# A softmax router kernel: its first three loads moved from the kernel block to the entry block

## The chip, the cores and the metric

The program runs on one core of one Trainium2 chip. The metric is the device time of one execution in microseconds (us). Three unprofiled executions of the kernel before took 86.51, 86.59 and 86.63 us, so its time is the median, 86.59 us. One more execution was recorded by the hardware profiler: its device time was 86.38 us, and from its first to its last recorded instruction it spans 85.1 us.

## What is computed

```python
def setup_inputs():
    batch, seq, dim = 16, 512, 1024
    num_loras = 8
    # x: (16, 512, 1024) float32, router_weights: (1024, 8) float32

def reference(x, router_weights):
    logits = np.matmul(x, router_weights)
    exp_logits = np.exp(logits - np.max(logits, axis=-1, keepdims=True))
    return (exp_logits / np.sum(exp_logits, axis=-1, keepdims=True)).astype(np.float32)
```

There are 16 x 512 = 8192 rows of 1024 numbers. Each row is multiplied with eight columns of weights, and a softmax is taken over the eight results. The input is 33.55 MB and the output 0.26 MB.

## The kernel before

**Tiling.** The rows are laid over 128 partitions so that each partition holds 64 consecutive rows of x. A "row" of the kernel, index j from 0 to 63, is therefore 128 rows of x, one from each partition. The tile `xa` (named x_all in the profile) keeps all of x in bf16, 64 rows of 1024 numbers in each partition. Nothing is ever loaded twice, and no load waits for a buffer.

**Loads.** Rows 0 to 3 come in as float32: SyncE (SP) issues two transfers of two rows each into `x_f32` (lines 133 to 138, recorded as line 134), and ScalarE (ACT) issues the load of the weights into `w8` (line 140). They are written inside a block that the tile framework closes and compiles at lines 146 and 147, and each has its own semaphore: `s_f[0]`, `s_f[1]` and `s_w`. Rows 4 to 62 and the pieces of row 63 come through GpSimd's (POOL's) queue, which casts to bf16 on the way (lines 170 and 183). They follow the list `LOADS = [4] * 13 + [2, 2, 2] + [1] * 5` without its first entry: twelve transfers of four rows, three of two, five of one, and at last row 63 in three pieces of its columns, `PIECES = [4, 2, 2]` (in units of 128 columns). Between the second and the third of them POOL builds the identity matrix and a filler tile (lines 174 to 180).

**Work on a row.** ACT casts the four float32 rows to bf16 (line 337). For each row TensorE (PE) transposes eight 128 x 128 blocks (lines 233 and 278, the latter for all repeated ones), VectorE (DVE) copies five of them out of PSUM and ACT three (lines 395 and 351), and PE multiplies the eight transposed blocks with the weights (line 265 for the repeated ones, which include two filler matmuls in every two rows). After each eight rows DVE and ACT do the softmax. The last four rows are finished one by one, and two stores by SP write the result (lines 161 and 163).

**What sets the order.** Every engine has its instructions written out by hand, with semaphores between them. SP waits for each load in turn and counts the rows that are in into `s_in` (lines 152 to 158); PE takes one from `s_in` ahead of each row (lines 214 and 277). ACT waits for `s_f[0]` ahead of the first cast and for `s_f[1]` ahead of the third (line 335).

**The start of the program.** It has three blocks in a row that every engine goes through, and two of them hold barriers of all five engines.

1. The entry block, recorded under line 520: POOL writes four small constants, and each engine executes a drain and then joins a barrier.
2. The kernel block: the two float32 loads on SP and the load of the weights on ACT, and nothing else that is recorded.
3. The end of the tile block, recorded under line 147: drains, a barrier, a clearing of semaphores by POOL, drains, a second barrier. Behind it come the hand-written instructions of all engines, on POOL the first of the casting loads.

In a barrier POOL collects the arrivals of all the engines and then releases them.

Of the kernel before, what the change touches and what calls it, by code (L numbers as in the profile page):

```python
# [11 lines left out]
def kernel(  # L12
# [6 lines left out]
    nc = tc.nc  # L19
# [112 lines left out]
    with tc.manual_schedule():  # L132
        early = [
            nc.sync.dma_start(
                out=x_f32[:, 2 * i:2 * i + 2, :], in_=x_rows[:, 2 * i:2 * i + 2, :]
            ).then_inc(s_f[i], 16)
            for i in range(2)
        ]
# [6 lines left out]
            tc.no_tile_sem_insts.add(t.ins.name)  # L145
    tc.close()
    tc.compile()  # L147


    sp = nc.sync  # L150
# [120 lines left out]
    for n in range(N):  # L271
        t = pe.transpose(w_ps[:, n, :], w8[:, :, n], ident[0:KO, 0:KO])  # L272
# [263 lines left out]
```

## Time and profile before

| What | Value |
|---|---|
| Device time, median of three | 86.59 us (86.51 to 86.63) |
| Device time of the profiled execution | 86.38 us |
| Span of the profiled execution | 85.1 us |
| PE busy | 63.7 us (75%) |
| DVE busy | 39.5 us (46%) |
| ACT busy | 37.9 us (45%) |
| POOL busy | 13.4 us (16%) |
| Granted TensorE clock | 1.000 over the whole span |
| The two float32 loads: issued | 0.74 to 1.60 us, on SP |
| The load of the weights: issued | 0.74 to 1.33 us, on ACT |
| First casting load on POOL: issued | 3.29 us |
| First cast of a float32 row on ACT | 6.79 us |

A profile is one execution. "Busy" counts an engine's compute instructions; issuing a DMA, waiting and branching are not counted. Times in the profile count from the first recorded instruction, here a drain on SP in the entry block. The profile page also shows the span in 40 equal slices of 2.13 us, with the busy share of each engine and of the sixteen DMA engines in tenths. The rate in GB/s counts the bytes as they are written to their destination: a load that casts float32 to bf16 reads twice the bytes that it writes.

### The profile page before, as it was taken

Reading aid. Unit: us, or ns where it says so; the run is one execution under the profiler, and the core shown is the slowest. Engines: PE = TensorE matmul, PEld = TensorE weight load, DVE = VectorE, ACT = ScalarE, POOL = GpSimd, SP = SyncE. Lnnn points to the kernel's source line nnn. Section 1 sums busy time; section 2 is a strip of 40 time slices with the busy share of each in tenths; the row PEclk is TensorE's granted clock in tenths of the full one; section 3 lists DMA queues with packets and bytes.
Section 4 is the critical chain, followed back from the end, with each engine's and each line's share of the span. In section 5 each row is a group of like instructions: output and inputs, shape, how many; then the busy total and the mean of one; then the engine's idle time right before and its main releaser. Section 6 shows DMA issues by size and latency. Waiting matters only on the chain. (4 is left out here: it accounts for less than half of the span.)

```text
span 85.1 us, 2926 instructions
## 1 busy us (share of the span) xinstructions
PE 63.7 (75%) x1094; PEld 52.1 (61%) x1094; DVE 39.5 (46%) x114; ACT 37.9 (45%) x81; POOL 13.4 (16%) x30
## 2 busy tenths in 40 slices
PE   0044759999994977949596895949597799999760
PEld 0042648788774755838474674837476588777650
DVE  0021412377574442845265362736257257665661
ACT  0049683356453352535245262525336246555470
POOL 0489999800000000000000000000000000000000
PEclk9999999999999999999999999999999999999999
DMA  3899999899989999999999999999999999999920
GB/s 58 347 420 308 239 189 243 185 247 189 243 185 239 193 227 204 239 193 231 200 227 204 227 204 227 204 227 204 227 204 204 216 216 216 199 208 211 191 104 23
DMA packets 3904, 18.12 MB, mean 213 GB/s; under 512 B 568, under 2 KB 1080, under 8 KB 2112
## 3 DMA queue, kind: packets, MB, share of 16 engines
q0 software_dynamic: 3312, 15.73, 90.5%
q1 hardware_dynamic: 576, 2.36, 7.2%
q10 hardware_dynamic: 16, 0.03, 0.3%
HBM read 33.59 MB, written 0.26 MB: 398 GB/s over the span
## 5 line engine op out<-in xcount | busy, mean ns | idle before, releaser
L351 ACT COPY xTs<-pts 128x384 bf16<-128x384 bf16 x63 | 30.0, 476 | 37.5 <-PE pts L278 37.1
L395 DVE COPY xTv<-ptv 128x640 bf16<-128x640 bf16 x63 | 31.0, 492 | 32.3 <-PE ptv L278 29.7
L278 PE MATMUL ptv<-identity,x_all 128*128 128x128 bf16 x311 | 28.7, 224 | 12.7 <-PEq L214 11.4
L278 PEld LDWEIGHTS ptv<-identity,x_all 128*128 (+1 forms) x311 | 18.8, 99 | 14.1 <-issue 13.9
L278 PE MATMUL pts<-identity,x_all 128*128 128x128 bf16 x186 | 21.3, 225 | 0.0
L265 PEld LDWEIGHTS lg<-w_bf,xTv 128*128 128x128 bf16 x305 | 15.6, 98 | 7.8 <-issue 1.1
L265 PE MATMUL spare<-filler 128*128 128x512 bf16 x61 | 19.5, 402 | 0.4
L265 PE MATMUL lg<-w_bf,xTv 128*128 128x8 bf16 x305 | 16.6, 167 | 0.0
L278 PEld LDWEIGHTS pts<-identity,x_all 128*128 x186 | 13.6, 101 | 0.0
L265 PE MATMUL lg<-w_bf,xTs 128*128 128x8 bf16 x183 | 13.2, 166 | 0.0
L170 POOL DMA_DIRECT2D x_all<-in_x_dram x20 | 10.7, 612 | 2.8 <-POOLq L147 2.8
L265 PEld LDWEIGHTS lg<-w_bf,xTs 128*128 128x128 bf16 x183 | 9.0, 96 | 0.0
L265 PEld LDWEIGHTS spare<-filler 128*128 128x128 bf16 x61 | 4.4, 101 | 2.5 <-issue 2.5
L272 PE MATMUL lg<-ident,w 8*128 8x8 f32 x8 | 1.0, 251 | 5.3 <-PEq L270 5.3
L272 PEld LDWEIGHTS lg<-ident,w 8*128 8x128 f32 x8 | 0.9, 197 | 5.3 <-issue 5.3
L415 DVE TENSOR_REDUCE mx<-lg 128x8 f32 x8 | 1.8, 225 | 5.0 <-DVEq L465 4.5
L337 ACT CAST x_all<-x_f 128x1024 bf16<-128x1024 f32 x4 | 4.0, 1044 | 0.0
L337 ACT ACT_TABLE_LOAD x1 | 1.3, 1283 | 5.5 <-ACTq L335 5.5
L386 DVE CAST identity<-ident 128x128 bf16<-128x128 f32 x1 | 0.5, 518 | 5.3 <-POOL ident L176 5.3
L340 ACT ACTIVATE ev<-ex 128x64 f32<-128x64 f32 x8 | 2.0, 256 | 1.6 <-DVE ex L415 0.9
L431 DVE TENSOR_REDUCE ssum<-ev 128x8 f32<-128x64 f32 x8 | 1.8, 220 | 0.1
L415 DVE TENSOR_TENSOR ex<-lg,mx 128x64 f32<-128x64 f32 x8 | 1.7, 217 | 0.0
(41 smaller groups left out, 16.0 us busy)
## 6 DMA issues: line engine op xcount, KB each, us to landing
x_all<-in_x_dram POOLq DMA_DIRECT2D x12, 1024.0 KB, 32.1
x_f<-in_x_dram SPq DMA_DIRECT2D x2, 1024.0 KB, 6.3
x_all<-in_x_dram POOLq DMA_DIRECT2D x3, 512.0 KB, 59.9
x_all<-in_x_dram POOLq DMA_DIRECT2D x5, 256.0 KB, 64.0
out_dram<-out_all SPq DMA_DIRECT2D x1, 208.0 KB, 1.9
x_all<-in_x_dram POOLq DMA_DIRECT2D x1, 128.0 KB, 65.6
x_all<-in_x_dram POOLq DMA_DIRECT2D x2, 64.0 KB, 65.3
out_dram<-out_all SPq DMA_DIRECT2D x1, 48.0 KB, 1.6
```

Of the source, the lines that this page charges most:

```text
L170: nc.gpsimd.dma_start(out=xa[:, first[i]:first[i] + r, :], in_=x_rows[:, first[i]:first[i] + r, :]).then_inc(s_ld[i], 16)
L265: return pe.matmul(spare, lhsT=filler[:, 0:P], rhs=filler, start=True, stop=True)
L272: t = pe.transpose(w_ps[:, n, :], w8[:, :, n], ident[0:KO, 0:KO])
L278: turn_like = pe.transpose(turn_ap(0, 0), xa[:, 0, 0:P], identity).ins
L337: act.copy(xa[:, k, :], x_f32[:, k, :]).then_inc(s_cast, 1)
L340: return act.activation(ev, ex, func=Exp).then_inc(s_ev, 1)
L351: act.copy(xTs[j % 2], pts[j % 2][:, 0:SN, :]).then_inc(s_c[j % 2], 1)
L386: dve.tensor_copy(out=identity, in_=ident).then_inc(s_idb, 1)
L395: dve.tensor_copy(out=xTv[j % 2], in_=ptv[j % 2][:, 0:VN, :]).then_inc(s_c[j % 2], 1)
L415: return dve.add_instruction(kind(name=f"I-{nc.next_id()}", engine=dve.engine, **k))
L431: dve.reduce_sum(ssum[:, :, 0], ev, axis=X).then_inc(s_d, 1)
```

## The change

The three load instructions stay as they are written. After the framework has compiled its block, they are taken out of the kernel block and put into the entry block, each ahead of its own engine's first drain there. The two loads on SP keep their order. Nothing else is touched: POOL's constants, the barriers, the semaphores and all that follows are as before.

```diff
--- before.py
+++ after.py
@@ -145,6 +145,21 @@
             tc.no_tile_sem_insts.add(t.ins.name)
     tc.close()
     tc.compile()
+
+
+    entry = nc.bb_map["main"].bb.instructions
+    body = next(
+        b.bb.instructions for b in nc.bb_map.values()
+        if any(i.name == early[0].ins.name for i in b.bb.instructions)
+    )
+    for t in early:
+        one = next(i for i in body if i.name == t.ins.name)
+        body.remove(one)
+        place_of = next(
+            k for k, i in enumerate(entry)
+            if i.engine == one.engine and isinstance(i, mybir.InstDrain)
+        )
+        entry.insert(place_of, one)
```

## The prediction

> **What bounds the kernel now.** I read the page's slices first, then the busy shares by stretch, then who waited at the end of the run, then the start instruction by instruction.
>
> The page, its rows of DMA and the queues:
>
> ```profile
> span 85.1 us, 2926 instructions
> ...
> DMA  3899999899989999999999999999999999999920
> GB/s 58 347 420 308 239 189 243 185 247 189 243 185 239 193 227 204 239 193 231 200 227 204 227 204 227 204 227 204 227 204 204 216 216 216 199 208 211 191 104 23
> ...
> q0 software_dynamic: 3312, 15.73, 90.5%
> ```
>
> The sixteen DMA engines are at 9 in almost every slice from the second to the 38th. POOL's casting queue (q0) alone fills 90.5% of their span. The busy shares by stretch say it more finely (the last two numbers of a line are the DMA share and the GB/s written):
>
> ```profile
> 0.00:1.50 1.50, 0.00 (x0) 0.00 (x0) 0.00 (x0) 0.00 (x0) 0.20 (x4) 1.00 0.00 0
> 1.50:2.50 1.00, 0.00 (x0) 0.00 (x0) 0.00 (x0) 0.00 (x0) 0.00 (x0) 1.00 0.90 188
> 2.50:3.50 1.00, 0.00 (x0) 0.00 (x0) 0.00 (x0) 0.00 (x0) 0.21 (x1) 1.00 0.85 328
> 3.50:7.20 3.70, 1.55 (x9) 1.05 (x9) 0.74 (x2) 1.69 (x2) 3.46 (x8) 1.00 1.06 438
> 7.20:12.00 4.80, 2.54 (x29) 2.40 (x30) 0.98 (x2) 4.04 (x6) 4.80 (x11) 1.00 1.04 217
> ...
> 50.00:70.00 20.00, 15.60 (x291) 12.77 (x287) 9.43 (x27) 8.03 (x19) 0.00 (x0) 1.00 1.04 214
> ```
>
> Nothing moves until 1.5 us. Then the float32 loads move at up to 438 GB/s, and from about 7.2 us the casting loads write 214 to 217 GB/s, which is 428 to 434 GB/s read: the same read rate. The share stays at 1.0 to 81 us, with no hole where the queues change over. The page's 33.59 MB read over those 79.5 us are 423 GB/s, so the time is a fixed stream at a fixed rate, plus what lies ahead of it (1.5 us) and behind it (some 4 us).
>
> That the end hangs on the stream is in the waits of SP, which counts in the loads:
>
> ```profile
> SPq L158 <- DMA x_all<-in_x_dram: 66.9, 20, 4.8
> ```
>
> SP waited for all of its 20 loads, 66.9 us in total. PE is not the limit: in 50 to 70 us it was busy for 15.60 of 20 us. The chain that ended last begins at 80.10 us with the transposes of row 62, ahead of which PE sat idle for 0.42 us waiting for `s_in` (line 214), and runs through row 63's pieces to the last store. That tail follows the last data; if the stream ends earlier, it starts earlier.
>
> So the question is what sets the stream's start. The start of the run in order of time:
>
> ```profile
> 0.74 0.59 ACTq L140 DMA_DIRECT2D w<-in_router_weights_dram  x1
> 0.74 0.86 SPq L134 DMA_DIRECT2D x_f<-in_x_dram  x2
> 3.29 1.21 POOL L170 DMA_DIRECT2D x_all<-in_x_dram  x2 [2.85 <-POOLq L147]
> ```
>
> and the instructions of lines 520 and 147 (counts, durations min/median/max in ns, first and last start):
>
> ```profile
> L520 SPq DRAIN  x1: 7/7/7, 0.0 to 0.0; - x1
> L520 POOLq DRAIN  x1: 184/184/184, 0.3 to 0.3; - x1
> ```
>
> ```profile
> L147 SPq DRAIN  x2: 7/68/128, 1.6 to 1.8; - x2
> ```
>
> SP is ready at 0.0 and waits 0.7 us in the entry barrier for POOL, whose constants and drain last to 0.3 + 0.18 = 0.5 us. Then SP issues, and in the first barrier of line 147 everyone else waits for SP.
>
> **What the Trainium skill says.**
> - "DMA: Bandwidth & Descriptors", section "Issuing engines are not separate DMA queues": transfers from SP, ACT and POOL run on the same 16 engines and interleave. The trace agrees: 438 GB/s of float32, then 2 x 217 of casting loads, never both in full. So the float32 bytes can't be hidden beside the others; only the idle time ahead of them can be removed.
> - The same page, "Latency and other measured facts": the first byte about 0.6 us after issue on the path of SP and ACT, about 1 us on POOL's. Here SP and ACT issue at 0.74 and the first records come after 1.5, at least 0.76 us, somewhat more. On POOL the gap is 3.29 to about 7.2 us, 3.9 us; while float32 data fills the engines, the trace doesn't say how much of it is queueing.
> - "Perfetto Trace Analysis", section "DMA Instruction — HWDGE (DVE, Sync)": the record of such an issue covers making the descriptors, not moving the data. The trace agrees: 0.86 us for two issues, while the first landing comes 4.7 us after its issue. The same section has one descriptor generator shared by the issuing engines, so SP's and ACT's issues may lengthen each other. Before, both began at 0.74, so the 0.59 and 0.86 us include that.
>
> **The change part by part.**
>
> 1. *The two float32 loads on SP.* Two issues, 0.383 and 0.426 us, 0.86 us with the gap, move from 0.74 to 0.0, where SP's drain stood. The stream's start moves by **-0.74 us**, and the end of the float32 bytes from about 7.3 to 6.56 us. Unknown is the price of such an issue as an engine's very first instruction. From below it is as before, +0 (no reason for less: no queue is emptier than before). From above I take a doubling of the first, +0.4. I choose 0.
>
> 2. *The weights' load on ACT*, 0.59 us, moves from 0.74 to 0.1 (ACT's drain there). On no path: PE's first transposes of weights at 5.33 wait for POOL's identity (done at 4.95 + 0.28 = 5.23). Cost and gain 0. ACT is in the barrier at 0.1 + 0.6 + a drain of 0.15 = 0.9 us, ahead of SP.
>
> 3. *The entry barrier now waits for SP.* Queued behind the two issues is SP's drain, and behind that all five engines. After the same two issues in line 147 SP's drain took 0.128 us, while the landings came microseconds later, so a drain does not wait for the data. SP arrives at 0.86 + 0.05 + 0.13 = 1.04 us instead of 0.0; POOL's 0.5 us is no longer last. From last arrival to release takes 0.2 us (0.5 to 0.7 here; 1.8 to 2.0 in line 147). Release: about 1.2 instead of 0.7, **+0.5 us** for the barrier alone.
>
> 4. *The first barrier of line 147 no longer waits for SP.* Without the issues each engine arrives within 0.15 us of its release (DVE's and PE's drains at 0.8 after 0.7), and 0.2 us later it is released: 1.2 + 0.15 + 0.2 = 1.55 instead of 2.0, **-0.45 us** for everyone. The rest (clearing, second barrier, POOL's way to line 170) keeps its 3.29 - 2.0 = 1.29 us, so POOL issues its first casting load at about 2.84, and identity, weights and PE's start move by the same 0.45.
>
> 5. *The change-over.* The float32 bytes end 0.74 us earlier, POOL's queue begins only 0.45 earlier. Before, there was no hole, so POOL's data was ready at 7.2 us or sooner. If it was just ready, and always takes 3.9 us from the issue, it comes at 2.84 + 3.9 = 6.74, and a hole of up to 6.74 - 6.56 = 0.18 us opens. If it was only queued behind float32 data, no hole opens. The gain of the stream is thus 0.56 to 0.74; I take the middle, **0.65 us**.
>
> 6. *The rest* moves with the stream: the first rows' casts and transposes sit in a stage where PE is idle half the time (2.54 of 4.80 us), hidden by the loads.
>
> Sum: span 85.1 - 0.65 = 84.4 us. Device time is about 1.3 us above the span in the profiled execution (86.38 against 85.1), on neither side touched by the change. Against the median of the unprofiled runs: 86.59 - 0.65 = **85.94 us**.
>
> **The rivals.**
> - *A: the stream moves by 0.5 to 0.8 us* (the sum): 85.94, own range 85.80 to 86.10. For it: a full DMA share from 3.5 to 81 us.
> - *B: part of it is lost at the start*, because the first issue as a first instruction is dearer by 0.2 to 0.4 us, or the hole at the change-over is larger: gain 0.25 to 0.5, so 86.2. For it: ACT's one small issue took 0.59 us against SP's 0.38, so issue times do vary.
> - *C: the end doesn't follow the stream's start*, or the loads start no earlier because the engines aren't ready for them: 86.59. Against it: 0.42 us of waiting for data right before the last chain; the engines' readiness at 0.0 isn't shown by the trace.
> - *D: slower.* The issues in the entry block are much dearer than 0.86 us and hold the entry barrier, and with it POOL's 90% of the bytes. POOL's start is at -0.45 + extra; from an extra of some 0.5 us (less the slack of point 5) the run is slower than before. At an extra of 1.0 us: POOL starts at 2.84 + 1.0 = 3.84, its data 0.55 us later than before, hence 87.1. Against it: the same instructions with the same neighbours took 0.86 us. A drain that waited for landing would be worse, but 0.128 us in line 147 speaks against it.
>
> **How the numbers follow.** Chances: A 0.72, B 0.13, C 0.07, D 0.08. The forecast is A's 85.94. About 0.2% of the time, 0.17 us, is what the measurement can tell from no change. A and B lie beyond it: faster 0.85; C same 0.07; D slower 0.08. The range takes in A and B: low, a gain of 0.74 plus 0.1 of spread among runs (86.51 to 86.63), 85.75; high, a gain of 0.25, 86.34.
>
> **What would show it.** In the changed profile: float32 issues at 0.0 and SP's drain at about 0.9; the waits of the others in the entry barrier at 1.0 to 1.1 us instead of SP's 0.7; first DMA share above 0 at about 0.8 instead of 1.5; POOL's first load at 2.84; written rate dropping from some 430 to 215 GB/s at 6.6 to 6.8 with or without a hole; the last chain starting near 79.45 instead of 80.10. The prediction is wrong if the issues take over 1.3 us, if POOL's first load isn't earlier than 3.29, or if the stream begins earlier and the last data doesn't come earlier.

## The result, and the profile after

The changed kernel takes 85.92 us (85.81 to 86.00, four executions) beside 86.61 us (86.51 to 86.74) for the kernel before: a ratio of 0.9919, 95% interval 0.9899 to 0.9938. That is 0.69 us less. The ratios here and below leave out executions over 1.5% slower than the fastest of the same kernel; this matters for the first experiment alone, whose ratio rests on 13 of its 22 executions and its median on all. The change adds 15 lines ahead of the hand-written part, so lines after 147 of the kernel before have numbers 15 higher here: the casting loads are line 185, the entry block is line 535.

The page of the changed kernel, rows of DMA and the casting queue:

```profile
span 84.7 us, 2926 instructions
...
DMA  5999999999999999999999999999999999999920
GB/s 122 416 430 244 224 194 240 190 240 194 228 201 232 201 228 205 224 209 224 209 221 213 217 217 209 224 201 232 194 240 190 207 215 215 205 207 213 162 101 23
...
q0 software_dynamic: 3312, 15.73, 90.9%
```

What differs clearly is the left end. The first slice has a DMA share of 5 instead of 3 and 122 GB/s instead of 58, and the row is 9 from then on. The start in order of time shows why:

```profile
0.00 0.86 SPq L134 DMA_DIRECT2D x_f<-in_x_dram  x2
0.12 0.58 ACTq L140 DMA_DIRECT2D w<-in_router_weights_dram  x1
...
2.83 1.21 POOL L185 DMA_DIRECT2D x_all<-in_x_dram  x2 [2.39 <-POOLq L147]
```

The float32 loads are issued at 0.0 instead of 0.74 us, at the same 0.86 us for both, and POOL's first casting load comes at 2.83 instead of 3.29. The barriers in between, as the instructions of lines 535 and 147 give them:

```profile
L535 SPq DRAIN  x1: 125/125/125, 0.9 to 0.9; - x1
L535 SPq EVENT_SEMAPHORE  x1: 17/17/17, 1.2 to 1.2; - x1
```

```profile
L147 SPq EVENT_SEMAPHORE  x2: 17/17/17, 1.5 to 2.3; - x2
```

SP's drain in the entry block now stands behind the two issues and takes 0.125 us; it doesn't wait for data, which starts to move only at 1.0 us and goes on for microseconds. The entry barrier lets SP go at 1.2 us instead of 0.7, and the two barriers of line 147 at 1.5 and 2.3 instead of 2.0 and 2.7. So the entry barrier lets go 0.5 us later than before, and the way from there through the next one is 1.0 us shorter.

The busy shares by stretch (last two numbers: DMA share and GB/s written):

```profile
0.90:1.00 0.10, 0.00 (x0) 0.00 (x0) 0.00 (x0) 0.00 (x0) 0.00 (x0) 1.00 0.00 0
1.00:1.10 0.10, 0.00 (x0) 0.00 (x0) 0.00 (x0) 0.00 (x0) 0.00 (x0) 1.00 3.33 573
1.10:1.50 0.40, 0.00 (x0) 0.00 (x0) 0.00 (x0) 0.00 (x0) 0.00 (x0) 1.00 1.49 246
1.50:1.75 0.25, 0.00 (x0) 0.00 (x0) 0.00 (x0) 0.00 (x0) 0.00 (x0) 1.00 0.00 0
...
6.60:6.80 0.20, 0.00 (x0) 0.00 (x0) 0.00 (x0) 0.20 (x1) 0.20 (x2) 1.00 1.38 287
6.80:7.00 0.20, 0.00 (x0) 0.00 (x0) 0.00 (x0) 0.20 (x1) 0.20 (x2) 1.00 0.98 205
```

A transfer is counted where it starts, so short stretches can exceed 1. The first bytes of x move at 1.0 us (before, by the trace's transfer records, the weights at 1.71 and x at 1.90); from 1.50 to 1.75 us nothing starts. The rate falls from float32 to casting loads at 6.6 to 6.8 us, with no hole. How far the stream is ahead, from its start to 20 us, before and after:

```profile
0.00:20.00 20.00, 12.09 (x148) 9.88 (x149) 5.80 (x16) 9.40 (x15) 13.44 (x30) 1.00 0.94 244
```

```profile
0.00:20.00 20.00, 12.44 (x165) 10.31 (x166) 5.95 (x17) 9.61 (x15) 13.44 (x30) 1.00 0.98 251
```

Seven GB/s more over 20 us are 140 KB, and at the 215 GB/s of the casting loads that is 0.65 us of lead (0.56 to 0.74, as both rates are rounded to 1 GB/s). The chain that ended last starts with the wait for row 62:

```profile
79.71 0.04 issue
79.75 0.44 PE ptv L293 x5
```

It starts 0.39 us earlier than the 80.10 of before. The two profiled executions differ by only 0.38 us in device time (86.38 and 86.00), where the medians differ by 0.69: before's profiled execution lies below all its unprofiled ones and after's at the top of its own. The traces show one reason. Each casting load ends with sixteen records of 4 bytes (368 for the 23 loads), as many as there are DMA engines; they are called closing records here and taken as one per engine, though a record doesn't name its engine. In the first casting load the middle one of the sixteen came 0.70 us earlier than before (11.58 instead of 12.28), the last one only 0.40 (12.02 instead of 12.42): after the change one engine was late in the profiled execution. The load has landed when all sixteen are through, at 2.83 + 9.6 = 12.4 us, by the view of line 185 at 2.8 us:

```profile
DMA to landing us min/median/max: 9.6/9.6/9.6
```

The last chain is read with that in mind.

### The profile page after: what moved, and what is told of

Read it like the earlier page. It is cut to its first block, busy times and chain, and to the rows that moved or that the text cites. A ratio compares the mean times of both kernels' runs of the same rounds, so it can differ in the third digit from the quotient of the medians.

```text
span 84.7 us, 2926 instructions
## 1 busy us (share of the span) xinstructions
PE 63.4 (75%) x1094; PEld 51.9 (61%) x1094; DVE 39.4 (47%) x114; ACT 37.9 (45%) x81; POOL 13.4 (16%) x30
## 5 line engine op out<-in xcount | busy, mean ns | idle before, releaser
L185 POOL DMA_DIRECT2D x_all<-in_x_dram x20 | 10.7, 615 | 2.4 <-POOLq L147 2.4
L198 POOL DMA_DIRECT2D x_all<-in_x_dram x3 | 1.7, 704 | 0.0
```

The lines of the kernel that those rows point to most:

```text
L185: nc.gpsimd.dma_start(out=xa[:, first[i]:first[i] + r, :], in_=x_rows[:, first[i]:first[i] + r, :]).then_inc(s_ld[i], 16)
L198: nc.gpsimd.dma_start(out=xa[:, J - 1, c], in_=x_rows[:, J - 1, c]).then_inc(s_z[i], 16)
```

## The experiments

Three questions were asked: whether it is the start of the float32 loads or the earlier start of everything else that gains, whether the weights' load matters, and how late POOL's first load may come. All times are beside the kernel before on the same chip, which took 86.53 to 86.61 us there.

**Only the float32 loads moved** (x_only_early).

```diff
-    for t in early:
+    for t in early[:2]:
         one = next(i for i in body if i.name == t.ins.name)
```

> Only the two float32 loads are in the entry block; the weights' load stays in the kernel block. SP issues at 0.0 as in the changed kernel, but ACT now issues behind the entry barrier (released at about 1.2), until 1.9, and the barrier of line 147 waits for it: POOL's first casting load at about 3.6 us, later than in both kernels (3.29 before, 2.83 changed). Theory S (what counts is when the DMA engines get their first bytes; POOL's loads only queue behind the float32 data): as the changed kernel, 85.9 us. Rival P (what counts is when POOL's queue starts, its data always 3.9 us or so behind its issue): 0.3 us slower than before, 86.9 us. Rival Q (the loads don't matter, all engines simply start earlier): as before or slower, 86.6 to 86.9.

Measured: 87.21 us, ratio 1.0046 (1.0023 to 1.0069). It is slower than before, although its first bytes move 0.9 us earlier. Twenty of its 22 executions took 87.0 to 87.5 us; the other two took 85.95 and 86.04, the time of the changed kernel, so the loss can also stay away. The start in order of time:

```profile
0.00 0.86 SPq L134 DMA_DIRECT2D x_f<-in_x_dram  x2
...
1.26 0.58 ACTq L140 DMA_DIRECT2D w<-in_router_weights_dram  x1
3.51 1.20 POOL L185 DMA_DIRECT2D x_all<-in_x_dram  x2 [3.07 <-POOLq L147]
```

ACT's issue now stands between the entry barrier and the first one of line 147 and holds the latter, so POOL is 0.68 us later than in the changed kernel. What that does shows from 7 to 10 us, this run first, the changed kernel below:

```profile
7.00:10.00 3.00, 3.00 (x30) 2.66 (x31) 0.99 (x3) 1.57 (x3) 3.00 (x6) 1.00 0.88 153
```

```profile
7.00:10.00 3.00, 2.16 (x25) 1.99 (x25) 0.98 (x2) 2.24 (x4) 3.00 (x7) 1.00 1.05 218
```

The casting loads write 153 GB/s instead of 218: 65 GB/s over 3 us are 195 KB, or 0.9 us at 215 GB/s, part of the 1.3 us by which the run is slower than the changed kernel. From 10 us on the rate is as in the others. Neither theory S (85.9) nor a proportional loss fits alone; rival P came nearest (86.9).

**Only the weights' load moved** (w_only_early).

```diff
-    for t in early:
+    for t in early[2:]:
```

> Only the weights' load is in the entry block. ACT holds the entry barrier until about 0.9, so it is released at about 1.05 instead of 0.66, and SP's float32 issues and POOL's first casting load both move back by 0.4 us (1.13 and 3.7). Theory S: 87.0 us, slower than before. Rival P: also 87.0. A rival in which the weights are what the start waits for: faster than before, 86.2 to 86.4.

Measured: 86.84 us, ratio 1.0030 (1.0019 to 1.0041). Slower, so the weights are not what the start waits for. ACT holds the entry barrier and SP issues at 1.14 instead of 0.74 us, but by the trace's transfer records the first float32 transfer starts at 2.15 instead of 1.90. The time rose by 0.29 us, which is nearer to the first transfer's 0.25 than to the issue's 0.40; the one profiled execution, at 87.00 the slowest of its seven, can't decide between them. POOL's load comes at 3.69 here, later than in the run before, and no 1.2 us are lost by it.

**The float32 loads behind the barriers** (x_after_barriers). An edit of the kernel before.

```diff
-        early = [
-            nc.sync.dma_start(
...
+        early = []
...
+    for i in range(2):
+        sp.dma_start(
+            out=x_f32[:, 2 * i:2 * i + 2, :], in_=x_rows[:, 2 * i:2 * i + 2, :]
+        ).then_inc(s_f[i], 16)
     for j in range(LOADS[0]):
         sp.wait_ge(s_cast, j + 1)
```

> The float32 loads are issued by SP behind the barriers of line 147, at about 2.6 us instead of 0.74; the weights stay where they were before. SP no longer holds the first barrier of line 147, ACT does, so POOL's first casting load comes at about 3.05, 0.24 us earlier than before. Theory S: no byte of x moves until 3.6 to 4 us instead of 1.9, so about 1.9 us slower than before, 88.5 us. Rival P: 0.24 us faster than before, 86.4 us. Rival Q: the same, 86.4 us.

Measured: 88.19 us, ratio 1.0188 (1.0175 to 1.0201). The stretches of its start:

```profile
0.00:3.40 3.40, 0.00 (x0) 0.00 (x0) 0.00 (x0) 0.00 (x0) 0.62 (x5) 1.00 0.03 10
3.40:4.40 1.00, 0.00 (x0) 0.00 (x0) 0.00 (x0) 0.00 (x0) 0.99 (x3) 1.00 1.03 254
```

Up to 3.4 us only the weights move. The first float32 transfer starts at 3.50, 1.60 us later than before, and the time rose by 1.64. POOL's load came earlier than before (2.98 instead of 3.29) and gained nothing. This rules out P and Q as the source of the gain: the start of the stream sets the time, here nearly one for one. In its trace the two queues also mix: casting transfers start at 7.19 us, and the last float32 transfer ends at 13.71.

**POOL's first load later by the building of the identity** (pool_late).

```diff
-        if i == 2:
+        if i == 0:
             nc.gpsimd.memset(ident, 0.0).then_inc(s_m, 1)
```

> The changed kernel, with POOL's building of the identity and the filler put ahead of its first casting load instead of behind the second: that load is issued about 1.2 us later, at 4.05, with all else in place. Theory S: POOL's loads have slack behind the float32 data, which fills the engines until 6.6 to 6.8; if their data needs 2.5 us or less from the issue, nothing changes, 85.9 us. Rival P: 1.2 us slower than the changed kernel, 87.1 us.

Measured: 87.08 us, ratio 1.0049 (1.0036 to 1.0062).

```profile
3.48 2.79 POOL L185 DMA_DIRECT2D x_all<-in_x_dram  x5
```

POOL's load moved by only 0.65 us, to 3.48, because POOL took part of the work into time in which it stood still before. Yet 1.2 us were lost. So the changed kernel does need POOL's load in time, and the loss is larger than the delay.

**The float32 loads early, the weights behind the barriers** (x_early_w_late).

```diff
-        early.append(
-            nc.scalar.dma_start(
-                out=w8, in_=router_weights.rearrange("(ko ki) n -> ko ki n", ko=KO)
-            ).then_inc(s_w, 16)
-        )
...
     act = nc.scalar
+    act.dma_start(
+        out=w8, in_=router_weights.rearrange("(ko ki) n -> ko ki n", ko=KO)
+    ).then_inc(s_w, 16)
```

> The float32 loads in the entry block as in the changed kernel, the weights' load behind the barriers of line 147, so that ACT no longer holds a barrier: POOL's first casting load at about 2.83 us again, as in the changed kernel, instead of the 3.51 of the run with the weights in the kernel block (87.21 us). Theory H (the stream's start sets the time, but POOL's load must be issued early enough to be ready before the float32 data ends; else its first transfers are slow and about 1.2 us are lost): 85.9 us. Rival W (it was the late weights' load itself, queued behind the float32 data, that cost the 1.2 us): 87.2 us or more.

Measured: 85.86 us, ratio 0.9926 (0.9907 to 0.9945). With the weights at 2.33 us, later than in the first experiment (1.26), the whole gain is back, and POOL's load is back at 2.82:

```profile
0.00 0.86 SPq L134 DMA_DIRECT2D x_f<-in_x_dram  x2
2.33 0.58 ACTq L344 DMA_DIRECT2D w<-in_router_weights_dram  x1
2.82 1.21 POOL L180 DMA_DIRECT2D x_all<-in_x_dram  x2 [2.38 <-POOLq L142]
```

In these runs the weights' load is worth nothing by itself; what matters is the barrier that its issue holds. Rival W falls.

**POOL's first load later in steps** (pool_by_0_2, pool_by_0_4, pool_by_5). Three runs put one memset of an unused tile of 704, 896 or 4096 columns ahead of the casting loads. Nothing else is changed; the first is shown.

```diff
+    scratch = sb("scratch", [P, 704], bf16)
...
+    nc.gpsimd.memset(scratch, 0.5)
     for i, r in enumerate(LOADS):
         if i:
             nc.gpsimd.dma_start(
```

> The changed kernel with one memset of an unused tile on POOL ahead of its first casting load, sized to issue that load about 0.2 us later (3.03 instead of 2.83). Theory H, a step: still within the slack (before the change the load came at 3.29 with the float32 data ending 0.74 later, that is at 2.55 in the changed kernel's time), or just over the step; 85.9 us, at most some runs at 87. Rival P (one for one): 86.1 us.

> The same with a longer memset, for about 0.4 us (3.23). With 0.65 us (3.48) the time was 87.08. Theory H, a step: either 85.9 or about 87.0, or runs of both kinds. Rival P': a loss in proportion that starts at once (1.2 us for 0.65): 86.6 us in all runs.

> The same with a memset of some 4 us, so that POOL's first load is issued near 7 us, when the float32 data has just ended. This measures the way from issue to the first casting transfer with nothing in front of it. If it is 1 us (as the Trainium skill's page DMA: Bandwidth & Descriptors says in Latency and other measured facts): first transfer near 8 us and 85.9 + 1.2 + 1.2 (slow first transfers) = 88.3 us. If it is 3.2 us as the runs with a late POOL suggest: first transfer near 10.2 us and 85.9 + 3.4 + 1.2 = 90.5 us.

Measured: 85.93 us (ratio 0.9939, 0.9919 to 0.9959) with the load at 2.95; 85.88 us (0.9923, 0.9906 to 0.9941) with the load at 3.12; 87.33 us (1.0110, 1.0076 to 1.0145) with the load at 5.78. The line of the second:

```profile
3.12 1.20 POOL L187 DMA_DIRECT2D x_all<-in_x_dram  x2
```

A step, then: nothing up to 3.12, 1.2 to 1.3 us at 3.48 to 3.51, and little more at 5.78. The last one also shows POOL's way with less in front of it:

```profile
5.78 0.67 POOL L187 DMA_DIRECT2D x_all<-in_x_dram  x1
```

```profile
7.00:7.10 0.10, 0.00 (x0) 0.00 (x0) 0.00 (x0) 0.10 (x1) 0.10 (x1) 1.00 0.00 0
7.10:7.20 0.10, 0.00 (x0) 0.00 (x0) 0.00 (x0) 0.10 (x1) 0.09 (x1) 1.00 1.94 246
```

Nothing starts from 7.0 to 7.1 and the casting data comes between 7.1 and 7.2, about 1.4 us after the issue. For the first 0.8 us of these the float32 data still moved at full rate, so the way over empty engines is not measured. Behind float32 data the same way took 3.7 us (2.83 to 6.53 in the changed kernel). The memset took 3.5 us and not 4, so the load came at 5.78 and not near 7, and neither sum of the expectation (88.3 and 90.5) came true. Its second figure, 3.2 us on an empty path, was wrong.

**The float32 rows cut differently** (split_1_3, split_3_1_late).

```diff
+    PARTS = [(0, 1), (1, 4)]
...
-                out=x_f32[:, 2 * i:2 * i + 2, :], in_=x_rows[:, 2 * i:2 * i + 2, :]
+                out=x_f32[:, lo:hi, :], in_=x_rows[:, lo:hi, :]
             ).then_inc(s_f[i], 16)
-            for i in range(2)
+            for i, (lo, hi) in enumerate(PARTS)
```

> The changed kernel with the four float32 rows cut as one row and three rows instead of two and two, the casts following; the same bytes in the same order, the same ends, POOL's first casting load at about 2.83. In the slow runs (POOL's load issued at 3.48 to 3.51) its data can be ready 1.4 us later, as the run with the longest memset showed, that is at 4.9, when the first float32 transfer was over (about 4.4) and the second under way; in the fast ones (issue at 2.83 to 3.12) it was ready at 4.2 to 4.5, with the first still under way. Theory B (POOL's queue must be ready before the last transfer of SP's queue begins): the first transfer is now over at about 3.2, so POOL comes too late with an issue at 2.83: 87.1 us. Rival E (it must only be ready some 2.2 us before the float32 data ends, however it is cut): 85.9 us.

> The run with POOL's building first (first casting load at 3.48, 87.08 us), with the four float32 rows cut as three rows and one row. The first float32 transfer is now over at about 5.6, after POOL's data can be ready (4.9). Theory B: the 1.2 us are not lost, 85.9 us. Rival E: 87.1 us.

The second has parts of three rows and one, on top of the run with POOL's load at 3.48. Measured: 86.03 us (0.9934, 0.9919 to 0.9949) and 86.88 us (1.0031, 1.0019 to 1.0043). Theory B is wrong in both: where the cut lies does not decide. Rival E's times (85.9 and 87.1) come nearer in both.

**The two float32 loads on two queues** (two_queues).

```diff
-            nc.sync.dma_start(
+            (nc.sync, nc.scalar)[i].dma_start(
                 out=x_f32[:, 2 * i:2 * i + 2, :], in_=x_rows[:, 2 * i:2 * i + 2, :]
...
-            nc.scalar.dma_start(
+            nc.sync.dma_start(
                 out=w8, in_=router_weights.rearrange("(ko ki) n -> ko ki n", ko=KO)
```

> The changed kernel with the second float32 load on ACT instead of SP, both in the entry block, and the weights' load on SP behind the first; meant to fill the engines faster at the start, where the changed kernel's DMA share was 0.93 and 0.82 of 1.0 in its first two microseconds of transfers. POOL's first casting load at about 3.0. If the slow first transfers overlap in two queues: up to 0.3 us faster than the changed kernel, 85.6 us. If the start is bound by the engines' first transfers themselves: 85.9 us. Theory B gives 87.1 us, since both last transfers are under way when POOL's data is ready.

Measured: 86.05 us, ratio 0.9946 (0.9930 to 0.9962). No gain over the changed kernel. By the transfer records the second queue's first transfer starts only at 2.97 us, so the two did not share the start, and whether two queues would speed it up stays open. Theory B is wrong here too.

**The kernel before, with POOL's load later** (before_pool_late). The same edit as in the fourth run, without the change.

> The kernel before, with POOL's building of the identity and the filler put ahead of its first casting load, so that this load is issued about 0.65 us later (3.94 instead of 3.29) and the float32 data ends where it did (7.2 to 7.5). In the runs so far the 1.2 us were lost where POOL's first load was issued less than about 3.5 us ahead of that end, and not where it was 3.7 us or more. Theory E (this lead alone decides, whatever the block in which the loads stand): the lead is now 3.4 us, so 1.2 us are lost, 87.7 us. Rival: the loss belongs to loads in the entry block; as before, 86.6 us.

Measured: 86.57 us, ratio 1.0000 (0.9991 to 1.0010). No loss, against theory E as it was put. Its load came at 3.94:

```profile
0.74 0.86 SPq L134 DMA_DIRECT2D x_f<-in_x_dram  x2
3.94 2.27 POOL L170 DMA_DIRECT2D x_all<-in_x_dram  x4
```

Set side by side, with "gap" the time from SP's first issue to POOL's first casting load; with the longest of the first sixteen casting transfers from the trace's transfer records (0.62 to 0.64 us is usual); with the time at which POOL's first casting load had landed; and with "rest", the device time of that profiled execution less the landing:

```
run               gap us  longest us  landed us  rest us  median time us
x_after_barriers   0.49      0.64        14.7      73.5    88.19
before             2.55      0.64        12.8      73.6    86.55
w_only_early       2.55      0.63        13.4      73.6    86.84
two_queues         2.80      0.62        12.3      73.5    86.05
split_1_3          2.82      0.64        12.2      73.6    86.03
x_early_w_late     2.82      0.63        12.3      73.6    85.86
after              2.83      0.62        12.4      73.6    85.92
pool_by_0_2        2.95      0.63        12.3      73.6    85.93
pool_by_0_4        3.12      0.63        12.4      73.6    85.88
before_pool_late   3.20      0.64        13.1      73.6    86.57
split_3_1_late     3.47      1.89        13.4      73.6    86.88
pool_late          3.48      1.55        13.5      73.6    87.08
x_only_early       3.51      2.09        13.6      73.6    87.21
pool_by_5          5.78      1.35        13.7      73.6    87.33
```

Where the gap was 3.20 us or less no early casting transfer was slow; where it was 3.47 or more some were, and 1.0 to 1.4 us were lost in the medians. The ordering was formed after the last run, so it describes the runs and was not tested by one. A rule that only kernels with the loads in the entry block can lose, and only with POOL's load past 3.1 us, fits as well. The two executions of x_only_early that lost nothing show that a gap of 3.5 us does not always cost.

The column "rest" is the same in all fourteen: once the first casting load has landed, the device time of the profiled execution is fixed to 0.1 us. So all of the gains and losses arise before that. How one slow transfer can cost so much shows best in split_3_1_late:

```profile
3.47 2.80 POOL L186 DMA_DIRECT2D x_all<-in_x_dram  x5
```

```profile
DMA to landing us min/median/max: 9.9/9.9/9.9
```

```profile
7.00:10.00 3.00, 0.64 (x7) 0.67 (x8) 0.00 (x0) 2.99 (x3) 3.00 (x7) 1.00 1.02 216
```

From 7 to 10 us it writes 216 GB/s, as good as the 218 of the changed kernel, and only one of its casting transfers of 8 KB took over 0.9 us, that of 1.89. Yet its first load landed 1.0 us later (13.4 instead of 12.4). The last closing record of that load came 1.25 us behind the middle one, and in the twelfth load, at 66 us, still 1.21 us behind. In the changed kernel's profile the same lag is 0.44 and 0.43. In these traces an engine that falls behind at the start stays behind, and each load is in only when the slowest engine is through. So what a run loses is how late the slowest engine is in that first load, and the rate of all sixteen need not show it. In pool_by_5 the middle one is late as well (12.90 us instead of 11.58).

## Why the prediction was right

Forecast 85.94 us, measured 85.92; forecast gain 0.65, measured 0.69.

1. *The float32 loads.* Issues at 0.0, both in 0.86 us: as put, with no extra price for being SP's first instructions. The first bytes were expected at about 0.8 us and came at 1.0. SP's issues take 0.86 us with or without ACT's beside them (0.86 also in x_early_w_late), so the two did not lengthen each other. That the gain comes from them is shown by x_early_w_late (85.86 with these loads alone moved ahead) and by the run with the loads behind the barriers: 1.60 us later in the first transfer, 1.64 us in time.
2. *The weights' load.* Costed at nothing, and worth nothing with the weights at 2.33 us (85.86). The prediction didn't see how much hangs on moving them along: left in the kernel block, their issue holds the barrier and the kernel is slower than before (87.21).
3. *The entry barrier.* Release forecast at about 1.2, measured 1.2, SP's drain 0.125 us against 0.13.
4. *The barriers of line 147.* First one at 1.55 forecast, 1.5 measured; POOL's first load at 2.84 forecast, 2.83 measured.
5. *The change-over.* Here the reason was not the right one. The prediction took 0.09 us off for a hole of up to 0.18 us between the queues. There is no hole, and POOL's load could come 0.29 us later still at no cost (85.88). Without that deduction the forecast would have been 85.85, which the measured 85.81 to 86.00 fit as well. That 0.65 came so near to 0.69 is therefore luck. What keeps the gain under 0.74 us, if anything does, the runs don't show.
6. *The rest* moved with the stream. The last chain was forecast near 79.45 and came at 79.71 in the one profiled execution, in which one engine was late (0.44 us behind the middle one, before 0.14).

The rivals: B's dearer issue did not occur, nor C. D, slower through a late POOL, is a real danger. It was put at an extra of some 0.5 us, where a loss in proportion would have used up the gain. The runs show an edge between 0.29 (nothing) and 0.64 (1.0 us); that the two places agree is partly luck, since the loss is not in proportion to the delay but a step of 1.0 to 1.4 us. Why some of the first casting transfers are then slow, up to three times as long as usual, is open. No run told apart the way in which the engines pick up the second queue from a disturbance of the memory reads.

No run beat the changed kernel beyond the intervals; 85.86 us with the weights last is the same time.

## What to carry to other kernels

In a kernel that is one long stream of loads, look for the first byte: an engine that is ready but waits in a start-up barrier can issue its loads ahead of it, and here the time followed the first transfer. Then follow every barrier that the moved issues now hold, or no longer hold, to the queue that carries the rest of the bytes: leaving one small load behind turned the same gain into a loss. Check the margin by delaying that queue in steps. And look at when the first load of that queue has landed as a whole, not only at the rate: in these fourteen profiles the landing alone fixed the end.

## What was not expected of the hardware

- POOL's first casting transfer came 3.15 to 4.2 us after its issue behind float32 data, and 1.4 us after it where float32 data filled only the first 0.8 us of the way. The Trainium skill's page "DMA: Bandwidth & Descriptors", section "Latency and other measured facts", gives about 1 us; no run here measures the way over empty engines, and the loaded one is far off.
- The first float32 transfer came 1.0 us after an issue at time 0 and 1.16 us after one at 0.74 us; the same section gives about 0.6 us.
- A delay of 0.36 us in the issue of one load (3.12 to 3.48) cost 1.2 us of run time, with transfers that took up to 1.55 us instead of 0.62.
- A single slow transfer of 1.89 us went with a run 1.0 us longer (split_3_1_late): the lag of one engine at the start (1.25 us) was still 1.21 us at 66 us.
